# Hybrid SSD and attention layer: the attention values projected for eight heads at a time

## The chip, the cores and the metric

The kernel runs on one core of a Trainium2 chip. The metric is the device time of one execution in microseconds (us), as the median of several runs. TensorE is called PE in the rows, its weight loads PEld, VectorE DVE, ScalarE ACT, GpSimd POOL, and SyncE, which issues most DMAs, SP.

## The reference: what is computed

One decoder layer on 512 tokens of width 1024, all in float32. The part that matters here:

```
h = rms_norm(x, norm_mix_w)
z, xbc, dt, q, k, v, f = split(h @ w_in)       # q, k, v: 16 heads of 64 columns
y_ssd = ssd_mixer(xbc, z, dt, ...)             # chunked scan, 2 groups of 8 heads
y_fox = softmax(qk/8 + cum_i - cum_j, causal) @ v   # "fox" attention, 16 heads
x = x + concat(y_ssd, y_fox) @ w_out
x = x + mlp(rms_norm(x, norm_ffn_w))           # w_up, conv, gate, w_down
```

## The kernel before, in words

Every float32 product is made of three matmuls of rounded operands (`mm3`, line 117): a weight tile is split into a high part `wh` (a CAST on ACT, line 110) and a low part `wl` (a subtraction on DVE or POOL, line 111), the activations `xh`, `xl` likewise, and high by high, high by low and low by high are added in one PSUM bank. `load_split` does the loading: a DMA of 128x1024 from SP's queue, the CAST, the subtraction. There are four buffers for split weights; `LOW_PART` says for each projection which engine subtracts ("d" DVE, "p" POOL).

The attention works on 16 heads in pairs, and on four groups of four heads. For a group, `qk_proj` projects q and k with `wide_block`: two passes over the four weight tiles, each pass with two banks of 128 tokens by 512 columns, all four split tiles being held until the second pass has used them. The values of a group were projected by `v_proj` with `token_block`: two weight tiles one after the other, two banks that each hold two blocks of 128 tokens by 256 columns, so each matmul has 256 columns. Its banks are called `pq`, those of `wide_block` `pw`, those of the output projection `po`.

Of a pair, `fox_qk` turns q and k (`qkT`) and writes `qs`, `ks`; of a head, `fox_bias` and `fox_scores` make the scores (`S`) and their exponentials (`prob`), `fox_turn` turns these (`pT`, copied by ACT to `pt`), and `fox_values` multiplies a pair's `pt` by the values `v` into the bank `o`, which ACT and DVE copy to `mfh` and `mfl`, the operands of the output projection. A bank of `po` is emptied by an addition to `x2` on DVE (line 263). There are three banks for all projections and four for the small tiles.

The order of the work is made by a scheduler, which places instructions on each engine by priority. What stands under `urgent()` (the scan of the SSD heads and all steps of the attention heads) goes first; the projections fill the gaps. The table `fillers` says behind which head a projection is released: "q1" is q and k of group 1, "v1" its values, "o0" and so on the output projection of attention pairs, "a0" and "a1" that of the second SSD group. The values of group 0 were projected before the attention began, beside the end of the second SSD scan (`yd`, `yo`, `st`, `yT` are its matmuls).

Of the kernel before, what the change touches and what calls it, by code (L numbers as in the profile page):

```python
# [8 lines left out]
F32 = mybir.dt.float32  # L9
F32R = mybir.dt.float32r  # L10
AF = mybir.ActivationFunctionType
# [4 lines left out]
P = 128  # L16
SEQ = 512
# [11 lines left out]
HD = 64  # L29
# [14 lines left out]
    "qk1": "dppd",  # L44
    "qk2": "pppd",
    "qk3": "dppd",
    "v0": "dd",
    "v1": "pd",
    "v2": "pd",
    "v3": "pd",  # L50
    "z1": "pdpd",
}
C_MIX, C_SCW, C_SCB, C_FCW, C_FCB, C_QW, C_KW, C_END = 0, 8, 56, 68, 200, 244, 245, 246
# [3 lines left out]
def tile_hybrid_layer(  # L57
# [37 lines left out]
    def low_part(key):  # L95
        order = LOW_PART.get(key, "p")
        n = taken.get(key, 0)
        taken[key] = n + 1
        return dve if order[n % len(order)] == "d" else pool
# [3 lines left out]
    def load_split(src, sub=None, four=True):  # L103
        r = wp.tile([P, 1024], F32, tag="wraw", name="wraw", bufs=3)
        nc.sync.dma_start(r, src)
        where = pa if four and loads[0] % 4 == 3 else wp
        loads[0] += 1
        h = where.tile([P, 1024], F32R, tag="wh", name="wh", bufs=3 if where is wp else 1)
        l = where.tile([P, 1024], F32R, tag="wl", name="wl", bufs=3 if where is wp else 1)
        act.copy(h, r)  # L110
        (sub or dve).tensor_tensor(out=l, in0=r, in1=raw(h), op=ALU.subtract)  # L111
        return h, l

    def mm3(o, ah, al, bh, bl, start, stop, grouped=True, keep=False):
        kw = {} if grouped else {"skip_group_check": True}
        for n, (a, b) in enumerate(((ah, bh), (ah, bl), (al, bh))):
            ins = pe.matmul(o, a, b, start=start and n == 0, stop=stop and n == 2, **kw)  # L117
            if keep:
                tc.keep_in_program_order(ins)

    def bank(name="g"):
        return pg.tile([P, 512], F32, tag="g", name=name)
# [201 lines left out]
        act.activation(eacs, tokS[:, 1, :, 0:16], AF.Exp)  # L324
        nc.sync.dma_start(dsk, ssd_d[0:1, :].to_broadcast([P, SSD_HEADS]))

    def token_block(src, key="tb"):
        tiles = [bank("pq") for _ in range(2)]
        for kh in range(2):
            h, l = load_split(src[kh], sub=low_part(key))  # L330
            for b in range(2):
                for j in range(4):
                    k = 4 * kh + j
                    for c in range(2):
                        tb = 2 * b + c
                        s = slice(tb * P, (tb + 1) * P)
                        mm3(
                            tiles[b][:, c * 256 : (c + 1) * 256], xh[:, k, s], xl[:, k, s],
                            h[:, j * 256 : (j + 1) * 256], l[:, j * 256 : (j + 1) * 256],
                            k == 0 and c == 0, k == NK - 1, grouped=False,  # L340
                        )
        return tiles

    def wide_block(src, key, use, behind=None):
        ws = []
        for b in range(2):
# [177 lines left out]
            dve.tensor_mul(tv, tv, mt[:, :, None].broadcast_to([P, 16, HD]))  # L524
        return tok[:, 0], tok[:, 1]

    def v_proj(gi):
        tiles = token_block(wv[gi], "v%d" % gi)
        v = pa.tile([P, NTB, 4, HD], F32, tag="v", name="v", bufs=2)
        for b in range(2):  # L530
            for c in range(2):
                tb = 2 * b + c
                o = tiles[b][:, c * 256 : (c + 1) * 256].rearrange("p (h d) -> p h d", d=HD)
                act.activation(v[:, tb], o, AF.Copy, scale=r[:, tb : tb + 1])
        return v

    LO, HI = slice(0, HD), slice(HD, P)
# [70 lines left out]
    def fox_turn(prob):  # L608
        where = {}
        for n, kbs in enumerate(((2,), (1, 3), (0,))):  # L610
            w = sum(SEQ - kb * P for kb in kbs)
            t = mbank("pT")
            pt = pf.tile([P, w], F32, tag="pt%d" % n, name="pt", bufs=4)
            w = 0
            for kb in kbs:
                where[kb] = (pt, w)
                for qb in range(kb, NTB):
                    o = QOFF[qb] + kb * P
                    pe.transpose(t[:, w : w + P], prob[:, o : o + P], ident)  # L619
                    w += P  # L620
            act.copy(pt, t[:, :w])
        return where

    def fox_values(pair, turned, v):
        o = po.tile([P, 512], F32, tag="o", name="o")
        for kb in range(NTB):
            for i, rows in ((1, HI), (0, LO)):
                pt, w = turned[i][kb]
                ins = pe.matmul(  # L629
                    o[rows, kb * P :], v[:, kb, (2 * pair + i) % 4, :], pt[:, w : w + SEQ - kb * P],  # L630
                    start=kb == 0, stop=kb == NTB - 1, skip_group_check=True,
                )
                if (kb, i) != (0, 1):
                    tc.keep_in_program_order(ins)
        mh = pf.tile([P, SEQ], F32R, tag="mfh", name="mfh", bufs=2)
        ml = pf.tile([P, SEQ], F32R, tag="mfl", name="mfl", bufs=2)
        act.copy(mh, o)
        dve.tensor_sub(ml, o, raw(mh))
        return mh, ml
# [16 lines left out]
    def project_v(g):  # L656
        vs[g] = v_proj(g)
# [2 lines left out]
    out_proj((0, 1), m0)  # L660
    with urgent():
        m1 = ssd_scan(1, *st1)
    project_v(0)
    pss_ctx.close()
    pf_ctx = ExitStack()
    pf = pf_ctx.enter_context(tc.tile_pool(name="pf", bufs=1, reuse_waits="tile"))
# [17 lines left out]

    def end_pair(p):
        with urgent():
            mf.append(fox_values(p, [turned.pop(n) for n in (2 * p, 2 * p + 1)], vs[p // 2]))

    fillers = {
        0: ["q1"], 3: ["v1"], 4: ["q2", "v2"], 5: ["o0"], 8: ["q3"], 9: ["a0", "o1"], 10: ["v3"], 12: ["o2"],  # L690
        15: ["a1"],
    }

    def fill(name):
        if name[0] == "a":
# [28 lines left out]
    for half in range(2):  # L724
        c = slice(half * 512, (half + 1) * 512)
        ks = slice(half * 4, half * 4 + 4)
        for tb in range(NTB):
            s = slice(tb * P, (tb + 1) * P)
            with urgent():
                xw = pf.tile([P, 512], F32, tag="xw" if tb % 2 else "cum", name="xw", bufs=2)  # L730
                (dve if (half, tb) == (1, 3) else pool).tensor_tensor(out=xw, in0=x2[:, tb, c], in1=nw[:, c], op=ALU.mult)
                t = mbank("hT")
                for j in range(4):
                    pe.transpose(t[:, j * P : (j + 1) * P], xw[:, j * P : (j + 1) * P], ident)
                tv = t.rearrange("p (j f) -> p j f", j=4)
                act.copy(hh[:, ks, s], tv)
                dve.tensor_sub(hl[:, ks, s], tv, raw(hh[:, ks, s]))
# [231 lines left out]
def _lay_out(i, np):  # L969
    w_in = i["w_in"][0]  # L970
    x = i["x"][0]

    def cols(v):
        return v.reshape(-1, 128).T

    def taps(v):
        t, n = v.shape
        return v.reshape(t, n // 128, 128).transpose(2, 1, 0).reshape(128, -1)

    dt, f = w_in[:, 2560:2576], w_in[:, 5648:5664]  # L980
    dtf = np.concatenate([dt, f], axis=1)
    qw, kw = i["fox_q_norm_w"][0], i["fox_k_norm_w"][0]
    pcol = np.concatenate(
        [
            cols(i["norm_mix_w"][0]), taps(i["ssd_conv_w"][0]), cols(i["ssd_conv_b"][0]),
            taps(i["ffn_conv_w"][0]), cols(i["ffn_conv_b"][0]), np.concatenate([qw, qw])[:, None],
            np.concatenate([kw, kw])[:, None],
        ],
        axis=1,
    )  # L990
    db, fb, al = i["ssd_dt_bias"][0], i["fox_f_bias"][0], i["ssd_a_log"][0]
    one = np.ones(16, np.float32)
    rows = [np.concatenate([one, -one]), np.concatenate([db, fb]), np.concatenate([al, np.zeros_like(al)])]
    pdtf = np.tile(np.stack(rows, axis=1), (4, 1))
    ftri = np.kron(np.triu(np.ones((4, 4), np.float32), 1), np.diag(np.repeat(np.float32([0, 1]), 16)))
    return {
        "x": x,
        "xT": x.T.reshape(8, 128, 512),
        "wdtf": dtf.reshape(8, 128, 32).transpose(1, 0, 2).reshape(128, 256),
        "wz": w_in[:, 0:1024].reshape(4, 2, 128, 2, 512).transpose(3, 0, 2, 1, 4).reshape(2, 4, 128, 1024),  # L1000
        "wxbc": _feature(w_in[:, 1024:2560], np),
        "wqk": w_in[:, 2576:4624].reshape(4, 2, 128, 2, 4, 256).transpose(4, 0, 2, 1, 3, 5).reshape(4, 4, 128, 1024),
        "wv": w_in[:, 4624:5648].reshape(2, 4, 128, 4, 256).transpose(3, 0, 2, 1, 4).reshape(4, 2, 128, 1024),
        "wout": _pairs(i["w_out"][0], np),
        "wup": _feature(i["w_up"][0], np),
        "wdown": i["w_down"][0].reshape(2, 11, 128, 2, 512).transpose(0, 3, 2, 1, 4).reshape(4, 128, 5632),
        "pcol": pcol,
        "norm_ffn_w": i["norm_ffn_w"],
        "pdtf": pdtf,
        "ftri": ftri,  # L1010
        "ssd_norm_w": i["ssd_norm_w"],
        "ssd_d": i["ssd_d"],
    }
# [19 lines left out]
```

## Time and profile before

| what | value |
|---|---|
| median of 3 runs | 803.82 us (803.39 to 804.31) |
| the profiled execution's own time | 802.56 us |
| its span, first to last instruction | 800.8 us |
| PE busy | 793.6 us (99%) |
| DVE, ACT, POOL busy | 554.8, 429.4, 262.5 us |
| granted TensorE clock | 0.999 of full speed |

The span is shorter than the execution's time by what lies ahead of the first and behind the last instruction. The recorded duration of a matmul reaches past the start of the next, since matmuls are pipelined; what one costs in a row of many is the distance from start to start, which the chain of waits and the timeline give.

### The profile page before, as it was taken

To read this page: it belongs to the slowest core of one execution; us is meant where nothing else is said; L and a number is where in the kernel's file an instruction comes from. 1 tells how busy PE (TensorE), PEld (TensorE's weight loads), DVE (VectorE), ACT (ScalarE), POOL (GpSimd) and SP (SyncE) were. 2 spreads that over 40 slices of the span, in tenths; PEclk is the share of its full clock that TensorE was granted. 3 is DMA by queue.
4 is the path that set the end of the run, shared out by engine and by line. 5 is a ranking of instruction groups with operands and counts; after the bars stand their busy time and mean duration, and the time that the engine had idled before them with its cause. 6 is when DMAs were issued, how large, how long until landed. Compare 5 with 4: busy or idle time off the path is not lost.

```text
span 800.8 us, 10949 instructions
## 1 busy us (share of the span) xinstructions
PE 793.6 (99%) x3975; PEld 655.3 (82%) x3975; DVE 554.8 (69%) x869; ACT 429.4 (54%) x787; POOL 262.5 (33%) x266
## 2 busy tenths in 40 slices
PE   9999999999999999999999999999999999999997
PEld 6888877878989798778887878888888888888886
DVE  4798998587567477657764577766766766778744
ACT  6557655472588686573751554443443443556531
POOL 0004362743448265225211424233333233133120
PEclk9999999999999999999999999999999999999999
DMA  8524322431334353323231363223223223299992
GB/s 322 186 74 164 104 80 80 146 131 53 112 113 126 98 154 97 106 66 123 77 117 52 129 188 106 84 100 106 86 99 106 88 98 105 85 256 191 211 191 92
DMA packets 31398, 98.13 MB, mean 123 GB/s; under 512 B 4016, under 2 KB 5104, under 8 KB 31344
## 3 DMA queue, kind: packets, MB, share of 16 engines
q1 hardware_dynamic: 27456, 85.38, 32.4%
q0 software_dynamic: 3456, 11.54, 8.0%
q8 instruction: 31, 0.51, 0.3%
q10 hardware_dynamic: 432, 0.52, 0.2%
q14 instruction: 23, 0.19, 0.1%
HBM read 91.56 MB, written 2.20 MB: 117 GB/s over the span
## 4 chain that ended last, share of the span: by engine, by line
PE 95%; DVE 3%; DMA 1%; issue 0%; ACT 0%; SPq 0%; DVEq 0%
PE up L117 30%; PE pw L117 16%; PE po L117 11%; PE pq L117 6%; PE Y L117 6%; PE g L117 5%; PE Z L117 4%; PE X L117 4%; PE o L629 2%; PE pT L619 2%; PE yd L458 2%; PE j L117 1%; PE S L596 1%; PE S L597 1%; DVE xs L397 1%; PE qkT L548 1%
## 5 line engine op out<-in xcount | busy, mean ns | idle before, releaser
L110 ACT CAST wh<-wraw 128x1024 fp32r<-128x1024 f32 x103 | 108.0, 1050 | 123.6 <-PE up L117 74.9
L117 PE MATMUL up<-hh,wh 128*128 128x512 f32 (+1 forms) x360 | 138.6, 385 | 0.3 <-DVE up L826 0.3
L117 PE MATMUL up<-hl,wh 128*128 128x512 f32 (+1 forms) x360 | 138.9, 386 | 0.0
L117 PE MATMUL up<-hh,wl 128*128 128x512 f32 (+1 forms) x360 | 138.5, 385 | 0.0
L111 DVE TENSOR_TENSOR wl<-wraw,wh 128x1024 fp32r<-128x1024 f32 x83 | 107.6, 1297 | 20.8 <-ACT wh L110 20.2
L111 POOL TENSOR_TENSOR wl<-wraw,wh 128x1024 fp32r<-128x1024 f32 x20 | 48.7, 2436 | 95.4 <-ACT wh L110 87.1
L117 PEld LDWEIGHTS up<-hh,wh 128*128 128x128 f32 x360 | 67.6, 188 | 14.2 <-PE up L117 0.7
L117 PEld LDWEIGHTS up<-hl,wh 128*128 128x128 f32 x360 | 67.6, 188 | 13.6 <-issue 0.2
L117 PEld LDWEIGHTS up<-hh,wl 128*128 128x128 f32 x360 | 67.6, 188 | 13.5 <-issue 0.2
L117 PE MATMUL pw<-wh,xh 128*128 128x512 f32 x192 | 77.4, 406 | 0.0
L117 PE MATMUL pw<-wl,xh 128*128 128x512 f32 x192 | 76.0, 396 | 0.0
L117 PE MATMUL pw<-wh,xl 128*128 128x512 f32 x192 | 75.3, 395 | 0.0
L826 DVE TENSOR_TENSOR up<-up,R 128x512 f32<-128x512 f32 x44 | 30.2, 691 | 59.3 <-PE up L117 57.6
L831 DVE SCALAR_TENSOR_TENSOR ua<-up,pc,ua 128x511 f32<-128x511 f32 (+1 forms) x88 | 66.6, 761 | 1.4
L598 DVE CUSTOM_DVE_ANT_0 prob<-S,prob 128x128 f32<-128x128 f32 (+1 forms) x64 | 30.3, 488 | 30.8 <-PE S L597 28.8
L787 ACT CAST wh<-T 128x1024 fp32r<-128x1024 f32 (+1 forms) x30 | 29.3, 977 | 36.8 <-PE Z L117 15.3
L788 DVE TENSOR_TENSOR wl<-T,wh 128x1024 fp32r<-128x1024 f32 (+1 forms) x30 | 33.7, 1133 | 19.1 <-ACT wh L787 18.8
L841 POOL TENSOR_TENSOR ua<-ua 128x512 f32<-128x512 f32 x11 | 15.0, 1363 | 91.0 <-DVE ua L831 91.0
L263 DVE TENSOR_TENSOR x<-po,x 128x512 f32<-128x512 f32 x48 | 32.7, 687 | 17.6 <-PE po L117 17.2
L602 ACT ACTIVATE prob<-prob,nm 128x128 f32<-128x128 f32 (+1 forms) x64 | 35.8, 561 | 16.8 <-DVE nm L598 16.4
L117 PEld LDWEIGHTS pw<-wh,xl 128*128 128x128 f32 x192 | 36.1, 188 | 7.4
L117 PEld LDWEIGHTS pw<-wh,xh 128*128 128x128 f32 x192 | 36.1, 188 | 7.3 <-issue 0.5
(235 smaller groups left out, 1908.7 us busy)
## 6 DMA issues: line engine op xcount, KB each, us to landing
wraw<-in_wup_dram SPq DMA_DIRECT2D x44, 512.0 KB, 3.3
T<-in_wdown_dram POOLq DMA_DIRECT2D x20, 512.0 KB, 7.6
wraw<-in_wqk_dram SPq DMA_DIRECT2D x16, 512.0 KB, 3.4
wraw<-in_wout_dram SPq DMA_DIRECT2D x16, 512.0 KB, 3.4
wraw<-in_wxbc_dram SPq DMA_DIRECT2D x11, 512.0 KB, 5.4
wraw<-in_wdown_dram SPq DMA_DIRECT2D x10, 512.0 KB, 3.7
T<-in_wdown_dram SPq DMA_DIRECT2D x10, 512.0 KB, 5.8
wraw<-in_wz_dram SPq DMA_DIRECT2D x8, 512.0 KB, 3.4
```

What stands on the lines that cost most here:

```text
L110: act.copy(h, r)
L111: (sub or dve).tensor_tensor(out=l, in0=r, in1=raw(h), op=ALU.subtract)
L117: ins = pe.matmul(o, a, b, start=start and n == 0, stop=stop and n == 2, **kw)
L263: dve.tensor_add(dst, banks[tb], dst)
L458: pe.matmul(yd[:, h * HD : (h + 1) * HD], sc[:, h, :], xdt[:, h * HD : (h + 1) * HD], start=True, stop=True)
L598: dve.tensor_tensor_reduce(out=p, in0=sps[:, :n], in1=p, scale=-1.0, scalar=-NEG, op0=ALU.add, op1=ALU.min, accum_out=nm[:, qb : qb + 1],)
L602: act.activation(p, p, AF.Exp, scale=-1.0, bias=nm[:, qb : qb + 1], accum_out=sm[:, qb : qb + 1])
L619: pe.transpose(t[:, w : w + P], prob[:, o : o + P], ident)
L787: act.copy(h[:, :n], src[:, :n])
L788: dve.tensor_tensor(out=l[:, :n], in0=src[:, :n], in1=raw(h[:, :n]), op=ALU.subtract)
L826: dve.tensor_mul(xp, o, R2)
L831: dve.scalar_tensor_tensor(out=a[:, s:], in0=xp[:, : SEQ - s], scalar=pc[:, cw + 2 - s : cw + 3 - s], in1=a[:, s:], op0=ALU.mult, op1=ALU.add,
```

## The change

`token_block` is removed. `v_proj` now makes the values of two groups (eight heads) at a time with `wide_block`: 512 columns in a matmul, two passes, four weight tiles held. The value tile is twice as wide, and there are two of them (`vs[p // 4]`) instead of four. The weights `wv` are laid out anew in memory, with the same bytes. The first values are no longer made before the attention but as its first filler, and the fillers are in another order. To make room, two of the three kinds of `pt` tiles have three buffers instead of four, and the tile `xw` of the following norm uses theirs.

```diff
-    "v0": "dd",
-    "v1": "pd",
-    "v2": "pd",
-    "v3": "pd",
+    "v0": "dpdp",
+    "v1": "dpdp",
...
-    def token_block(src, key="tb"):
...
-    def v_proj(gi):
-        tiles = token_block(wv[gi], "v%d" % gi)
-        v = pa.tile([P, NTB, 4, HD], F32, tag="v", name="v", bufs=2)
-        for b in range(2):
-            for c in range(2):
-                tb = 2 * b + c
-                o = tiles[b][:, c * 256 : (c + 1) * 256].rearrange("p (h d) -> p h d", d=HD)
-                act.activation(v[:, tb], o, AF.Copy, scale=r[:, tb : tb + 1])
+    def v_proj(both):
+        v = pa.tile([P, NTB, 8, HD], F32, tag="v", name="v", bufs=2)
+
+        def take(tb, o):
+            act.activation(v[:, tb], o.rearrange("p (h d) -> p h d", d=HD), AF.Copy, scale=r[:, tb : tb + 1])
+
+        wide_block(wv[both], "v%d" % both, take)
         return v
...
-            pt = pf.tile([P, w], F32, tag="pt%d" % n, name="pt", bufs=4)
+            pt = pf.tile([P, w], F32, tag="pt%d" % n, name="pt", bufs=4 if n == 0 else 3)
...
-    project_v(0)
     pss_ctx.close()
...
-    fillers = {
-        0: ["q1"], 3: ["v1"], 4: ["q2", "v2"], 5: ["o0"], 8: ["q3"], 9: ["a0", "o1"], 10: ["v3"], 12: ["o2"],
-        15: ["a1"],
-    }
+    fillers = {0: ["v0"], 1: ["q1"], 3: ["q2"], 5: ["v1"], 7: ["o0"], 8: ["q3"], 9: ["a0", "o1"], 12: ["o2"], 15: ["a1"]}
...
-                xw = pf.tile([P, 512], F32, tag="xw" if tb % 2 else "cum", name="xw", bufs=2)
+                xw = pf.tile([P, 512], F32, tag="pt1" if tb % 2 else "pt2", name="xw", bufs=3)
```

How the order of instructions moves is shown at three places; numbers behind names tell tiles apart, and line numbers of after are lower by two here and by some twenty further down.

PE at the beginning of the first value projection, of before: `po` is the output projection of the first SSD group, `yT` a step of the second SSD scan.

```order
L117 MATMUL po_1614<-wl_1576,msh_696 128x512
L117 MATMUL po_1614<-wh_1575,msl_697 128x512
L117 MATMUL pq_1859<-wh_1863,xh_93 128x256
L117 MATMUL pq_1859<-wl_1864,xh_93 128x256
L117 MATMUL pq_1859<-wh_1863,xl_94 128x256
```

The same place of after:

```order
L115 MATMUL po_1614<-wl_1576,msh_696 128x512
L115 MATMUL po_1614<-wh_1575,msl_697 128x512
L115 MATMUL pw_1982<-wh_1986,xh_93 128x512
L115 MATMUL pw_1982<-wl_1987,xh_93 128x512
L115 MATMUL pw_1982<-wh_1986,xl_94 128x512
```

The values follow the same output projection in both; although they are a filler of the attention now, the scheduler puts them beside the end of the scan again, in matmuls of 512 columns. There are 384 matmuls `pq` in before and 192 more `pw` in after, and no other matmul is added or removed.

SP's queue from there on, of before; `wraw` are weight loads (by the name of what they read: `wv` values, `wqk` q and k, `wout` output projection), `cum` the bias of a head, `ks` the second half of a pair's k operand.

```order
L105 DMA wraw<-in_wv_dram 128x1024 x2
L105 DMA wraw<-in_wqk_dram 128x1024 x4
L105 DMA wraw<-in_wv_dram 128x1024 x2
L568 DMA cum<-cf_d 128x512 x2
L105 DMA wraw<-in_wqk_dram 128x1024
L568 DMA cum<-cf_d 128x512 x4
L563 DMA ks<-ks 64x1024
L105 DMA wraw<-in_wqk_dram 128x1024 x2
L563 DMA ks<-ks 64x1024
```

Of after:

```order
L103 DMA wraw<-in_wv_dram 128x1024 x4
L103 DMA wraw<-in_wqk_dram 128x1024 x3
L548 DMA cum<-cf_d 128x512 x4
L103 DMA wraw<-in_wqk_dram 128x1024
L548 DMA cum<-cf_d 128x512 x2
L103 DMA wraw<-in_wqk_dram 128x1024 x3
L543 DMA ks<-ks 64x1024 x2
L548 DMA cum<-cf_d 128x512
L103 DMA wraw<-in_wqk_dram 128x1024
L548 DMA cum<-cf_d 128x512
```

Four value tiles are loaded at once, the second group's q and k come behind them, and the third pair's `ks` with them. Counted on PE, 437 matmuls of 512 columns in `po` and `pw` stand between the first scores of head 4 and the last of the last pair's `o` in after; in before 389 of them and 192 of 256 columns stand there. The scores, `pT`, `qkT` and `o` between them are the same in number.

PE behind the last pair's `o`, of before. The output projection of the last pairs there is `po_4475` and the banks that follow; `mfh_4465` is the last pair's operand, `mfh_4300` that of the pair before it.

```order
L117 MATMUL po_4475<-wh_4471,mfl_4466 128x512
L117 MATMUL po_4483<-wh_4471,mfh_4300 128x512
L117 MATMUL po_4483<-wl_4472,mfh_4300 128x512
L117 MATMUL po_4483<-wh_4471,mfl_4301 128x512
L117 MATMUL po_4483<-wh_4471,mfh_4465 128x512
L117 MATMUL po_4483<-wl_4472,mfh_4465 128x512
L117 MATMUL po_4483<-wh_4471,mfl_4466 128x512
L117 MATMUL po_4491<-wh_4471,mfh_4300 128x512
```

Of after, where the last pair's operand is `mfh_4263` and `mfl_4264` and the pair before it has `mfh_4098`:

```order
L115 MATMUL po_4289<-wh_4269,mfl_4099 128x512
L115 MATMUL po_4273<-wh_4269,mfh_4263 128x512
L115 MATMUL po_4273<-wl_4270,mfh_4263 128x512
L115 MATMUL po_4281<-wh_4269,mfh_4263 128x512
L115 MATMUL po_4281<-wl_4270,mfh_4263 128x512
L115 MATMUL po_4289<-wh_4269,mfh_4263 128x512
L115 MATMUL po_4289<-wl_4270,mfh_4263 128x512
L115 MATMUL po_4273<-wh_4269,mfl_4264 128x512
L115 MATMUL po_4281<-wh_4269,mfl_4264 128x512
L115 MATMUL po_4289<-wh_4269,mfl_4264 128x512
L115 MATMUL po_4297<-wh_4269,mfh_4098 128x512
```

In before a bank is finished before the next is begun, and the next but two stands 13 matmuls behind it; 26 matmuls on other operands stand between `o` and the first that reads `mfh_4465`. In after three matmuls stand between `o` and the first that reads `mfh_4263`, the three banks are finished one behind the other, and `po_4297`, which reuses the bank of `po_4273`, stands three places behind the last matmul of that bank.

## Rows read from the trace of the kernel before

**Rows 1.** The page: span, busy time of each engine, and the granted clock by slices.

```profile
span 800.8 us, 10949 instructions
...
PE 793.6 (99%) x3975; PEld 655.3 (82%) x3975; DVE 554.8 (69%) x869; ACT 429.4 (54%) x787; POOL 262.5 (33%) x266
...
PEclk9999999999999999999999999999999999999999
```

**Rows 2.** The waits, PE alone: total us, times, longest.

```profile
PE g L201 <- DVE mhalf L137: 1.0, 1, 1.0
PE g L211 <- ACT xh L188: 0.7, 1, 0.7
PE up L117 <- DVE up L826: 0.3, 1, 0.3
PE yT L491 <- DVE y L488: 0.2, 1, 0.2
```

**Rows 3.** Busy time by stretches: length, PE, PEld, DVE, ACT, POOL, clock, DMA.

```profile
100.00:150.00 50.00, 49.80 (x254) 39.79 (x253) 43.26 (x54) 29.57 (x73) 26.91 (x18) 1.00 0.26 90
...
199.00:216.00 17.00, 17.00 (x137) 16.30 (x136) 9.29 (x14) 7.70 (x15) 5.56 (x3) 1.00 0.34 117
...
262.00:330.00 68.00, 68.00 (x408) 57.44 (x405) 45.03 (x108) 49.84 (x110) 31.83 (x42) 1.00 0.37 110
330.00:404.00 74.00, 74.00 (x434) 61.27 (x433) 46.88 (x102) 44.66 (x93) 21.75 (x29) 1.00 0.32 101
```

**Rows 4.** Groups by form: one of the three `pq`, of 128 each.

```profile
L117 PE MATMUL pq<-wh,xh 128*128 128x256 f32 x128 | 37.0, 289 | 0.0
```

**Rows 5.** The chain of waits: start, us, what, for unbroken runs of matmuls.

```profile
187.80 7.23 PE po L117 x31
...
205.18 7.37 PE pq L117 x62
...
282.12 3.93 PE pw L117 x17
...
353.82 4.81 PE pw L117 x21
...
398.93 2.27 PE pq L117 x19
...
420.62 1.09 PE pT L619 x10
...
467.95 223.28 PE up L117 x984
```

**Rows 6.** Timeline of PE about a group of transposes: start, us.

```profile
127.99 0.60 PE L374 MATMUL xT<-ident,xs 128*128 128x128 f32 x4
128.35 0.48 PE L117 MATMUL pw<-wh,xh 128*128 128x512 f32 x1
128.66 0.40 PE L117 MATMUL pw<-wl,xh 128*128 128x512 f32 x1
```

**Rows 7.** Groups of ACT, DVE and POOL from 199 to 450 us.

```profile
L110 ACT CAST wh<-wraw 128x1024 fp32r<-128x1024 f32 x33 | 34.5, 1048 | 26.3 <-PE po L117 18.5 <-POOL xw L731 4.5 <-PE pw L117 2.9
L512 ACT ACTIVATE tok<-pw,r 128x512 f32<-128x512 f32 x12 | 8.3, 688 | 1.7 <-PE pw L117 1.5
L534 ACT ACTIVATE v<-pq,r 128x256 f32<-128x256 f32 x16 | 6.7, 472 | 6.5 <-PE pq L117 6.5
...
L111 DVE TENSOR_TENSOR wl<-wraw,wh 128x1024 fp32r<-128x1024 f32 x19 | 24.8, 1303 | 7.5 <-ACT wh L110 7.4
...
L111 POOL TENSOR_TENSOR wl<-wraw,wh 128x1024 fp32r<-128x1024 f32 x14 | 33.8, 2415 | 72.8 <-ACT wh L110 64.4 <-DVE x L263 7.4 <-DVE nm L598 1.0
```

**Rows 8.** DMA issues of the value weights: KB each, median us to landing.

```profile
wraw<-in_wv_dram SPq DMA_DIRECT2D x8, 512.0 KB, 4.2
```

**Rows 9.** Timeline where a `po` bank is emptied: PE's last matmul, DVE's addition.

```profile
434.94 0.40 PE L117 MATMUL po<-wh,msl 128*128 128x512 f32 x1
...
435.17 0.40 PE L117 MATMUL po<-wh,mfh 128*128 128x512 f32 x1
...
435.37 0.69 DVE L263 TENSOR_TENSOR x<-po,x 128x512 f32<-128x512 f32 x1 [0.71 <-PE po L117]
```

**Rows 10.** Timelines behind the last `o`: PE's next matmuls, then the copies.

```profile
429.74 0.50 PE L117 MATMUL po<-wl,msh 128*128 128x512 f32 x1
430.08 0.39 PE L117 MATMUL po<-wh,msl 128*128 128x512 f32 x1
430.31 0.39 PE L117 MATMUL po<-wh,msh 128*128 128x512 f32 x1
430.54 0.40 PE L117 MATMUL po<-wl,msh 128*128 128x512 f32 x1
...
429.86 0.59 ACT L637 CAST mfh<-o 128x512 fp32r<-128x512 f32 x1 [6.91 <-PE o L629]
...
430.48 0.69 DVE L638 TENSOR_TENSOR mfl<-o,mfh 128x512 fp32r<-128x512 f32 x1 [2.47 <-ACT mfh L637]
```

**Rows 11.** Timeline of PE, the first scores of head 4.

```profile
265.98 0.22 PE L596 MATMUL S<-ks,qs 128*128 128x128 f32 x1
```

More of the change, by code (lines that the diff above doesn't have):

```diff
@@ L325, in dt_f @@
         nc.sync.dma_start(dsk, ssd_d[0:1, :].to_broadcast([P, SSD_HEADS]))
-    def token_block(src, key="tb"):
-        tiles = [bank("pq") for _ in range(2)]
-        for kh in range(2):
-            h, l = load_split(src[kh], sub=low_part(key))
-            for b in range(2):
-                for j in range(4):
-                    k = 4 * kh + j
-                    for c in range(2):
-                        tb = 2 * b + c
[L336 to L342, printed above, removed]
     def wide_block(src, key, use, behind=None):
@@ L525, in qk_proj @@
         return tok[:, 0], tok[:, 1]
-    def v_proj(gi):
-        tiles = token_block(wv[gi], "v%d" % gi)
-        v = pa.tile([P, NTB, 4, HD], F32, tag="v", name="v", bufs=2)
-        for b in range(2):
-            for c in range(2):
-                tb = 2 * b + c
-                o = tiles[b][:, c * 256 : (c + 1) * 256].rearrange("p (h d) -> p h d", d=HD)
-                act.activation(v[:, tb], o, AF.Copy, scale=r[:, tb : tb + 1])
+    def v_proj(both):
[3 more added lines that the diff above has]
+        wide_block(wv[both], "v%d" % both, take)
         return v
@@ L629, in fox_values @@
                 ins = pe.matmul(
-                    o[rows, kb * P :], v[:, kb, (2 * pair + i) % 4, :], pt[:, w : w + SEQ - kb * P],
+                    o[rows, kb * P :], v[:, kb, (2 * pair + i) % 8, :], pt[:, w : w + SEQ - kb * P],
                     start=kb == 0, stop=kb == NTB - 1, skip_group_check=True,
@@ L686, in end_pair @@
         with urgent():
-            mf.append(fox_values(p, [turned.pop(n) for n in (2 * p, 2 * p + 1)], vs[p // 2]))
-    fillers = {
-        0: ["q1"], 3: ["v1"], 4: ["q2", "v2"], 5: ["o0"], 8: ["q3"], 9: ["a0", "o1"], 10: ["v3"], 12: ["o2"],
-        15: ["a1"],
-    }
+            mf.append(fox_values(p, [turned.pop(n) for n in (2 * p, 2 * p + 1)], vs[p // 4]))
+    fillers = {0: ["v0"], 1: ["q1"], 3: ["q2"], 5: ["v1"], 7: ["o0"], 8: ["q3"], 9: ["a0", "o1"], 12: ["o2"], 15: ["a1"]}
     def fill(name):
@@ L1002, in _lay_out @@
         "wqk": w_in[:, 2576:4624].reshape(4, 2, 128, 2, 4, 256).transpose(4, 0, 2, 1, 3, 5).reshape(4, 4, 128, 1024),
-        "wv": w_in[:, 4624:5648].reshape(2, 4, 128, 4, 256).transpose(3, 0, 2, 1, 4).reshape(4, 2, 128, 1024),
+        "wv": w_in[:, 4624:5648].reshape(4, 2, 128, 2, 512).transpose(3, 0, 2, 1, 4).reshape(2, 4, 128, 1024),
         "wout": _pairs(i["w_out"][0], np),
```

## The prediction

> **What bounds the kernel now.** I read the page first: the span is 800.8 us and PE is busy for 793.6 of it, while DVE, the next, is at 69%; the granted clock is full in every slice (2.4 GHz, the upper of its two levels) [rows 1]. A busy PE can still be a PE that waits inside its instructions, so I read the waits of PE next: in the whole span it waited four times, 2.2 us in all; by their lines two of the waits belong to the start (the warm-up and the first projection), and only 0.2 us (a `yT` of the scan) and 0.3 us (the first `up`) come later [rows 2]. The stretches say the same: from 199 to 404 us, where all value projections lie, PE is never idle, while ACT is busy for 49.84 of 68 us and for 44.66 of 74 us and DVE for 45.03 and 46.88 [rows 3]. So in the part that changes, PE's own instructions are the time. What is taken from PE's stream is gained; what is taken from DVE, ACT, POOL or the DMAs is worth nothing as long as it is not late; and every new wait of PE is lost in full.
>
> **The matmuls.** The recorded 289 ns of a `pq` matmul [rows 4] overlap its neighbours and can't be multiplied. What counts is the chain's unbroken runs, by length over number: `pq` 7.37/62 = 118.9 ns and 2.27/19 = 119.5; `pw` 4.81/21 = 229.0 and 3.93/17 = 231.2; the same shape in `po` 7.23/31 = 233.2, and in `up` 223.28/984 = 226.9 [rows 5]. There were 3 x 128 = 384 `pq` [rows 4], and 192 more `pw` take their place. I take 119 and 230: 384 x 0.119 = 45.70 us go, 192 x 0.230 = 44.16 us come, a gain of 1.54 us. Two narrow matmuls cost 238, a wide one 230: the columns are the same and take the same time, only 8 ns of fixed cost per pair go. Bounds: 118.9 against 233.2 gives 4.6 ns per pair, 0.9 us; 119.5 against 226.9 gives 12.1 ns, 2.3 us. I stay at 1.54, since the blocks of values will stand where the `pw` rows were taken.
>
> The Trainium skill (TensorE: Matmul & The Clock Gate, Back-to-back issue gap) gives the isolated gap of a matmul at the full clock as N/2.4 + 2.5 ns, so a fixed part of 2.5 ns; an estimate by it is 2.5 ns per pair, 0.5 us in all. The trace disagrees: 119 and 230 ns leave a fixed part of 8 ns.
>
> **The breaks between kinds of matmul.** I looked whether each group of small transposes between wide matmuls costs a penalty, for the order has four groups less by my count. Four transposes and the wide matmul behind them take 128.66 - 127.99 = 0.67 us [rows 6]; at 1.09/10 = 0.11 us a transpose in a run of ten [rows 5] and 0.23 for the matmul it is 0.67 without any penalty. So nothing is gained there.
>
> **Weights, their loads and splits.** Eight loads of 512 KB stay eight, 4.2 us to landing [rows 8], but four are issued at once and the q and k of the next group stand behind them on SP, and the `ks` copies of a pair behind those. A first pass uses a weight tile in 12 matmuls, 2.8 us; a tile is split in 1.05 us (ACT) plus 1.30 (DVE) or 2.42 (POOL) [rows 7]. Alternating "dpdp" keeps each engine below one split per 2.8 us. One subtraction moves from DVE to POOL in sum, ahead of a PE that does not ask for it before the tile's turn. I cost this at nothing; its cover is the earlier block on PE, and without it a split that came a whole POOL step late would cost 2.4 us at a block's start.
>
> **The evictions.** 16 activations of 0.472 us become 8 of the size of `tok`, 0.688 [rows 7]: 7.6 us of ACT become 5.5. ACT has a quarter of its time free there [rows 3], so nothing on the path. A `token_block` bank was full 24 matmuls ahead of the other; the two banks of a wide pass are full together, but so they are for q and k, whose evictions are two activations each and made PE wait nowhere [rows 2]. Nothing.
>
> **The buffers.** `pt` with three buffers instead of four: a pair's two tiles are freed when its `o` is done, two heads before the third buffer is wanted again. `xw` gets three buffers for two. Nothing.
>
> **The tail.** The order shows one new squeeze, behind the last `o`. First the copies: in before the next matmul stands at 429.74, the copy to `mfh` ends at 429.86 + 0.59 = 430.45 and the fourth matmul starts at 430.54 [rows 10]. In after three matmuls stand between, so the first that needs `mfh` comes just in time; it needs `mfl` six matmuls later, and this ended at 431.17, before 429.74 + 9 x 0.233 = 431.8. No wait. Then the banks: a bank's last matmul starts at 434.94, the addition that empties it ends at 435.37 + 0.69 = 436.06 [rows 9], 1.12 us later. In after the matmul that takes the bank again stands three places behind, 3 x 0.233 = 0.70 us. PE waits 0.42 us, from where nothing hides it: all behind it on PE is pushed by as much. Bounds: nothing if the additions start earlier than in [rows 9]; 0.69 more if another addition stands ahead on DVE, 1.1 us.
>
> **The second scan.** Around 100 to 150 us DVE is busy for 43.26 of 50 us, and the 0.2 us wait lies there [rows 2, 3]. The scheduler has shifted the steps of the scan against the matmuls by some places either way, a matmul being 0.23 us. A few of these steps had little room; I take nothing, with 0.2 us to gain, and to lose as much as three places at two steps, 1.4 us.
>
> **The sum.** -1.54 + 0.42 = -1.1 us. The profiled execution took 802.56 us, 1.26 below the median of the runs shown; the change should move both alike: 801.4 for such an execution, 802.7 for the median. That is 0.14%; a change of less than 0.2% (1.6 us) I call no change, which is about what a measurement of this kernel can tell.
>
> **The rivals.**
> *The wide matmuls run as well as those of `up`.* If the values run at 226.9 ns, or the narrow ones cost more among the heads than in the runs that I divided, the gain is up to 2.3 us, with 0.2 us from the scan and no wait at the tail 2.5 us: 801.3 us. For it: `up` has the same shape and reaches it over 984 matmuls [rows 5]. Against it: no run of `pw` does. It needs 10.5 ns per pair (2.0 us less 0.42) to pass the 1.6 us, or 8.4 ns without the wait. Chance 0.34.
> *Nothing is gained.* The fixed part is 2.5 ns per pair as by the rule, or 4.6 as by the slowest `po` run, 0.5 to 0.9 us, and the wait at the tail and a place or two in the scan take it back: 803.8 us. For it: the wait at the tail is in the order. Chance 0.14.
> *Slower: the attention heads run out of room.* Two wide blocks, values and q and k of group 1, now stand ahead of the third pair, so head 4 starts later, and its remaining 12 heads have less time. In before its first scores start at 265.98 [rows 11] and the last `o` ends at 429.74 [rows 10], 163.8 us; PE work in between falls from 389 wide and 192 narrow matmuls (112.3 us) to 437 wide (100.5), 11.8 us less. If the chain of the heads through ACT, DVE and POOL can't go faster than it did, PE stands idle for what is missing, at most 11.8 us: 814.5 us. It decides for slower from 2.7 us on. Against it: PE never waited for a head [rows 2], ACT is busy for 73% and 60% of the time there, and 8% more of it still fits [rows 3]. For it: ACT's queue is held up in order, its CASTs waited 18.5 us for `po` matmuls to free the weight buffers [rows 7], and what is behind a CAST are the exponentials and copies that a head needs. Chance 0.09.
>
> **How the numbers follow.** The forecast, 802.7 us, has 0.43; its own range is 802.2 to 803.4. Faster by over 0.2% is the first rival and a little of the forecast's lower edge, 0.36. Slower by over 0.2% is the third, 0.09. The rest is 0.55. The range runs from the first rival, 801.2, to where two of the small waits of scan and tail (1.4 and 0.7) are lost with the smallest gain, 804.6; outside lie most of the third rival and the end of the first.
>
> **What would show it.** The matmuls `pq` are gone and `pw` has 768, in runs of 229 to 231 ns. PE's waits stay few; a new one of about 0.4 us stands at a `po` matmul that waits for `x` (the addition), just behind the last `o`. No wait of PE for a split tile, for `mfh` or for `S`. ACT loses 2 us. The granted clock stays full. I am wrong if PE waits for more than 1 us between 199 and 404 us, or if runs of `pw` in the value blocks are outside 227 to 233 ns.

## The result: slower by a quarter of a per cent

The changed kernel took 804.60 us in the median of 20 runs (802.02 to 806.25) against 802.31 us of 20 runs of the kernel before, the three shown ahead included: a ratio of 1.0024 (1.0014 to 1.0033). In two later comparisons with before the same kernel stood at 1.0009 (0.9995 to 1.0022, so no change is not excluded there) and 1.0025 (1.0013 to 1.0038). The forecast, 802.7 us, was wrong: the sum had a gain of 1.1 us, and the medians show a loss of 0.6 to 2.7 us. That 804.60 lies at the upper end of the prediction's range says nothing for it: the range was reckoned from 803.82 us, the median of three runs of before. Reckoned from the 802.31 us of 20 runs it ends at 803.1.

The page of the profiled execution (803.65 us) answers to [rows 1]:

```profile
span 801.9 us, 10562 instructions
...
PE 792.6 (99%) x3783; PEld 644.6 (80%) x3783; DVE 560.9 (70%) x868; ACT 427.3 (53%) x779; POOL 258.3 (32%) x267
...
PEclk9999999999999999999999999999999999999999
```

The 192 matmuls are gone (3975 to 3783) and PE is busy for 1.0 us less, but the span is 1.1 us longer. So PE waits for longer; its waits answer to [rows 2]:

```profile
PE st L452 <- DVE xdt L450: 1.5, 1, 1.5
PE g L199 <- DVE mhalf L135: 1.0, 1, 1.0
PE g L115 <- ACT wh L181: 0.9, 1, 0.9
PE yT L472 <- DVE y L469: 0.4, 1, 0.4
PE po L115 <- DVE x L261: 0.3, 1, 0.3
...
```

The new and largest wait, 1.5 us at an `st` (the matmul of a scan step's new state, which reads `xdt`, a product that DVE makes for it), is not in the part of the program that the diff touches: it stands at 110 us, in the scan of the first SSD group, some 90 us ahead of the first value projection. The wait at a `po` for `x` is the predicted one at the tail. The wait of `up` for DVE [rows 2] is gone.

The stretches that answer to [rows 3], and one more, 404 to 450 us, in which the last heads lie (columns as there):

```profile
100.00:150.00 50.00, 48.15 (x246) 38.35 (x245) 43.78 (x56) 30.14 (x74) 22.20 (x18) 1.00 0.26 85
199.00:216.00 17.00, 17.00 (x80) 13.77 (x80) 8.88 (x12) 5.42 (x9) 5.50 (x7) 1.00 0.28 94
262.00:330.00 68.00, 68.00 (x354) 54.92 (x353) 41.98 (x88) 45.37 (x91) 32.47 (x33) 1.00 0.37 110
330.00:404.00 74.00, 74.00 (x395) 58.94 (x394) 54.31 (x121) 48.33 (x107) 27.84 (x41) 1.00 0.34 100
404.00:450.00 46.00, 45.59 (x243) 35.35 (x240) 30.72 (x60) 20.20 (x42) 11.60 (x8) 1.00 0.23 69
```

Where the values are, from 199 to 404 us, PE is never idle, as before. It stands still for 1.85 us between 100 and 150 us, where it stood still for 0.20 [rows 3], and for 0.41 us in the last stretch.

### The profile page after: what moved, and what is told of

It reads as the page before. It is cut to its first block, busy times and chain, and to the rows that moved or that the text cites. A ratio compares the mean times of both kernels' runs of the same rounds, so it can differ in the third digit from the quotient of the medians.

```text
span 801.9 us, 10562 instructions
## 1 busy us (share of the span) xinstructions
PE 792.6 (99%) x3783; PEld 644.6 (80%) x3783; DVE 560.9 (70%) x868; ACT 427.3 (53%) x779; POOL 258.3 (32%) x267
## 4 chain that ended last, share of the span: by engine, by line
PE 91%; DVE 4%; DMA 2%; ACT 1%; issue 1%; SPq 0%; POOL 0%; DVEq 0%; POOLq 0%; ACTq 0%
PE up L115 30%; PE pw L115 20%; PE po L115 11%; PE Y L115 6%; PE X L115 4%; PE Z L115 4%; PE g L115 3%; PE o L609 2%; PE pT L599 2%; PE j L115 1%; PE S L576 1%; PE yd L439 1%; PE S L577 1%; DMA sc<-cs_d 1%; PE qkT L528 1%
## 5 line engine op out<-in xcount | busy, mean ns | idle before, releaser
L115 PE MATMUL pw<-wl,xh 128*128 128x512 f32 x256 | 101.5, 396 | 0.0
L115 PE MATMUL pw<-wh,xh 128*128 128x512 f32 x256 | 101.2, 402 | 0.0
L115 PE MATMUL pw<-wh,xl 128*128 128x512 f32 x256 | 101.2, 397 | 0.0
L109 POOL TENSOR_TENSOR wl<-wraw,wh 128x1024 fp32r<-128x1024 f32 x21 | 51.0, 2429 | 75.0 <-ACT wh L108 75.0
L115 PEld LDWEIGHTS pw<-wl,xh 128*128 128x128 f32 x256 | 48.2, 188 | 9.9 <-issue 0.7
L115 PEld LDWEIGHTS pw<-wh,xl 128*128 128x128 f32 x256 | 48.1, 188 | 9.8 <-issue 0.2
L115 PEld LDWEIGHTS pw<-wh,xh 128*128 128x128 f32 x256 | 48.1, 188 | 9.6 <-issue 0.5
```

## A table by stages

The runs of one kernel differ by up to 4 us, and the traces show where: ahead of the first matmul `j` (about 23 us; `j` is the bank of the projections that end the kernel's start). Behind it, profiles of one kernel agree within 0.6 us. So I divided every profile at three starts: the first `j`, the first matmul of the values, the last `po`. All in us; the last column is the sum of the three stages behind `j`.

| kernel | start to `j` | `j` to values | values to last `po` | last `po` to end | behind `j` |
|---|---|---|---|---|---|
| before | 23.07 | 176.38 | 248.40 | 352.94 | 777.72 |
| before, longer warm-up | 21.23 | 176.57 | 248.39 | 352.99 | 777.95 |
| after | 23.12 | 180.37 | 245.39 | 353.00 | 778.76 |
| after, 2nd profile | 21.83 | 180.27 | 245.91 | 353.03 | 779.21 |
| after, 3rd profile | 24.11 | 180.28 | 245.38 | 352.96 | 778.62 |
| after, longer warm-up | 22.43 | 180.30 | 245.38 | 352.92 | 778.60 |
| after, z1 exchanged | 24.84 | 179.77 | 245.37 | 352.95 | 778.09 |
| after, heads' reach 1500 | 21.98 | 176.28 | 249.19 | 352.85 | 778.32 |
| before, reach 2250 | 24.60 | 180.68 | 246.08 | 353.00 | 779.76 |
| narrow values, new places | 23.22 | 176.26 | 253.27 | 352.92 | 782.45 |
| reach 1500, q3 first | 22.92 | 176.26 | 247.79 | 353.04 | 777.09 |
| the same, longer warm-up | 22.19 | 176.28 | 247.79 | 353.04 | 777.11 |
| heads still earlier, longer warm-up | 22.26 | 176.27 | 247.90 | 353.12 | 777.29 |
| after, z1's third subtraction on DVE | 23.05 | 178.94 | 254.65 | 352.92 | 786.50 |

One thing must be known to read it: in the kernels with 179.7 to 180.7 us in the second stage, the first value matmul stands behind 16 `yd` and four `yT` that elsewhere stand behind it. Twenty small matmuls at 0.11 us [rows 5] are 2.2 us, which are to be moved from the second stage to the third. With this, after loses 180.3 - 2.2 - 176.4 = 1.7 us ahead of the values and gains 248.4 - (245.4 + 2.2) = 0.8 us behind them, 0.5 us less in one of its four profiles (the second, where a score waits for a `ks` copy); in sum it is 0.9 to 1.5 us longer behind `j`.

## The experiments

**Theory A** says that the loss comes from the order of the start and the first scan. The scheduler puts what stands under `urgent()` ahead by `AHEAD` = 2000 places. The changed program is shorter, and ahead of the steps that start the later heads (numbers 8 and up) 96 to 192 matmuls fewer stand; so the same 2000 places reach further towards the program's start, and from some length on the order of PE's first rows, of SP's loads and of the whole first scan becomes another one. In the programs' order that is seen row by row: the kernel before has one early order for 1000, 1500 and 2000 places, and for 2250 and 2500 PE's rows up to the first value matmul are those of after; after with 1500 has the early order of before, also when only the steps of heads 8 and up get the 1500, and it keeps its own when only heads 0 to 3 get them. **Theory B** says that the wide blocks or the new places of the fillers cost the time where they stand.

**1. Only the heads' reach shortened, in the changed kernel.**

```diff
     def start_head(n):
         qs, ks = pairs[n // 2]
-        with urgent():
+        with tc.high_priority(1500):
```

> The changed kernel, but the steps that start a head are put ahead by 1500 places instead of 2000. Its order of instructions then equals that of the kernel before on all engines up to the first value projection. Theory A (the loss is the new order of the start and the first scan, which cost 2.0 us in the profiles between 100 and 112 us; the wide values gain 1.7 us where they stand): the wait of st for xdt (1.5 us) is gone and the kernel takes 2 us less than the changed one, so 0.5 us less than before to equal, a ratio of 0.999 to 1.000. Theory B (the wide blocks or their new places cost the time, between 199 and 450 us): it stays 1.5 to 2.3 us above before, a ratio of 1.002 to 1.003.

803.45 us, a ratio of 1.0008 (0.9992 to 1.0024). The wait of `st` is gone and the second stage is that of before, 176.28 us: here theory A holds. But the total did not fall by 2 us; three waits now stand in the last heads' stretch that before does not have:

```profile
PE S L576 <- DVE x L261: 0.9, 1, 0.9
PE po L115 <- ACT mfh L617: 0.7, 1, 0.7
PE po L115 <- DVE x L261: 0.3, 1, 0.3
```

**2. Only the reach lengthened, in the kernel before.**

```diff
-AHEAD = 2000
+AHEAD = 2250
```

> The kernel before with all urgent steps put ahead by 2250 places instead of 2000, nothing else; values in 256 columns at their old places. Its order then equals that of the changed kernel up to the first value projection. Theory A: st waits for xdt by about 1.5 us near 110 us and the kernel is slower than before by 2.0 to 2.8 us, a ratio of 1.0025 to 1.0035. Theory B: no wait that counts, a ratio of 0.9995 to 1.0005.

805.61 us, 1.0032 (1.0017 to 1.0047), with the values as narrow and as placed as in before. The wait:

```profile
PE st L471 <- DVE xdt L469: 1.8, 1, 1.8
```

Behind `j` it is 2.04 us longer than before, and nearly all of it ahead of the values: 180.68 - 2.2 - 176.38 = 2.1 us. The early order of after alone makes the kernel before slower by 2 us behind `j`: for the scan theory A is shown, without any change of the values.

**3. Narrow values at the new places, with the new buffers.** The values are made by `token_block` again, two groups one behind the other into a tile of eight heads; fillers and buffers are those of after. This program is long enough to keep the early order of before.

```diff
-        wide_block(wv[both], "v%d" % both, take)
+        for g in range(2):
+            tiles = token_block(wv[2 * both + g], "v%d" % both)
```

> The changed kernel with its places, buffers and value tiles of eight heads, but the values in matmuls of 256 columns again (384 instead of 192). The longer program keeps the order of before up to the first values. Theory A: no wait of st, no gain in columns, at the tail up to 0.5 us: 0 to 0.7 us slower than before, a ratio of 1.000 to 1.001. Theory B, if the places cost: 1.9 us and the 1.7 us of the columns on top, 1.0025 to 1.0045; if only the width of the blocks costs: 1.000.

808.36 us, 1.0074 (1.0053 to 1.0095), more than either theory allowed. The third stage is 4.9 us longer than before. Over half of that is one place where the scheduler has put `o` and `qkT` in turns (nine changes between the two kinds in this program, one in before, three in after); PE's timeline there:

```profile
294.21 1.07 PE L628 MATMUL o<-pt,v 128*64 128x512 f32 x2
295.21 0.33 PE L547 MATMUL qkT<-ident,tok 128*128 128x128 f32 x1
...
299.63 0.44 PE L547 MATMUL qkT<-ident,tok 128*128 128x128 f32 x2
```

From 294.21 to 299.63 us are 5.4 us for a pair's 16 `o` and four `qkT`; the last pair's 16 `o` in after take 2.3 us (435.06 to 437.37, below) and four transposes 0.44. So this cost 2.7 us. The rest, 2.2 us, goes with the same three waits at the last heads as in the first run. What follows is that the new places are not free, and that this run can't price the columns, since its order among the heads is another one than the first run's.

**4. The changed kernel again.**

> The changed kernel once more beside the others, so that all are compared on one chip: a ratio of 1.0024 by both theories.

803.61 us, 1.0009 (0.9995 to 1.0022), less than the 1.0024 expected; behind `j` 779.21 us. In this profile a score of the last heads waits for the copy of `ks` by DMA, which no other profile of after shows:

```profile
407.64 0.30 PE L576 MATMUL S<-ks,qs 128*128 128x128 f32 x1 [0.33 <-DMA ks<-ks]
```

By the medians, 803.45 and 803.61 us, the first run is not faster than after beyond the noise: what it gains in the scan it loses at the last heads.

**5. Reach 1500 and q3 ahead of o0.** Why should the last heads cost something? In after head 4 starts at 284.72 us (265.98 before, [rows 11]):

```profile
284.72 0.22 PE L576 MATMUL S<-ks,qs 128*128 128x128 f32 x1
```

The heads then catch up, but the last `o` starts at 437.16 us instead of 429.54, when 42 matmuls of the output projection are left instead of 71. So I released q and k of the last four heads earlier, and gave the reach of 1500 to all urgent steps, where the first run gave it to the starts of heads alone:

```diff
-AHEAD = 2000
+AHEAD = 1500
-    ... 7: ["o0"], 8: ["q3"], ...
+    ... 7: ["q3"], 8: ["o0"], ...
```

> The changed kernel with all urgent steps put ahead by 1500 places (the start and first scan then have the order of before, as in the first run) and, new, with the fillers q3 and o0 exchanged: q and k of the last group are released at head 7, the output projection o0 at head 8. By its order the last pair's o then has 71 matmuls of the output projection behind it, as in before, where the changed kernel has 42. Theory A, now with two parts (scan order 2.0 us, tail 1.0 to 2.4 us because the last heads come when the fillers are used up, columns a gain of 1.7 us): no wait of PE for st, S, mfh or x, and counted from 30 us on 1.7 us less than before, 0.9978 to 0.999 as a ratio. Theory B (wide blocks or their places cost something between 199 and 404 us whatever the tail): 0 to 1 us above before, 1.000 to 1.001.

802.04 us, 0.9999 (0.9986 to 1.0012), not the 0.9978 to 0.999 expected. Behind `j` it is 0.63 us shorter than before and 1.23 shorter than the first run, so the last heads have a part besides the scan; but of the columns' gain (1.6 us by the chain, below) only 0.63 is left. One wait of a `po` stays, at 398 us:

```profile
PE po L115 <- ACT mfh L617: 0.4, 1, 0.4
```

**6. The same with a longer warm-up.**

```diff
-WARM = 8
+WARM = 11
```

> The run just above with 11 instead of 8 warm-up matmuls at the start, which work on constants; the order is otherwise the same. In the traces so far the first matmuls that need data run at 0.43 us from start to start instead of 0.23 for 0 to 8 us, after PE stood still for 0.6 to 1.1 us between 5.5 and 7.5 us, and this alone moves everything behind it by -1.2 to +1.6 us from run to run. If the pause brings it, the longer warm-up shortens the pause and the runs lie closer together and about 1 us lower than those of the kernel just above; if not, the first data matmul only starts later and the time is the same or up to 0.5 us longer, with the same spread of 3 to 4 us.

800.69 us, 0.9986 (0.9974 to 0.9997), the one version that is below both kernels; 11 runs lie within 2.7 us (the 12 of the fifth within 4.2). Behind `j` it is the fifth run to 0.02 us. The gain came as expected, but not by a shorter pause: ahead of its data matmuls PE waits longer here than in the profile of the fifth run (1.1 us for an `xh`, where that has 0.5 for a `wh`).

**7. The changed kernel a third time.**

> The changed kernel a third time, beside the two above: 1.0009 to 1.0024 by the two comparisons so far; the runs above should be 3 us lower by theory A, 1 us by theory B.

804.42 us, 1.0025 (1.0013 to 1.0038), 2.4 us above the fifth run beside it, between the 1 us of theory B and the 3 of theory A.

**8. What holds `xdt` up: DVE's queue or POOL?** In after DVE takes 3.74 us for two pieces of `xs` ahead of the `xdt` that `st` waits for:

```profile
104.17 3.74 DVE L378 SCALAR_TENSOR_TENSOR xs<-xp,half_w,xs 128x511 f32<-128x511 f32 x2
107.83 0.68 DVE L475 TENSOR_TENSOR msl<-yT,msh 128x512 fp32r<-128x512 f32 x1
108.44 0.73 DVE L378 SCALAR_TENSOR_TENSOR xs<-xp,half_w,xs 128x509 f32<-128x509 f32 x1
109.09 0.68 DVE L442 TENSOR_TENSOR y<-yd,y 128x512 f32<-128x512 f32 x1
109.69 0.98 DVE L450 TENSOR_TENSOR xdt<-xdt,dte 128x512 f32<-128x512 f32 x1
```

Beside them POOL, and then PE:

```profile
104.97 2.40 POOL L109 TENSOR_TENSOR wl<-wraw,wh 128x1024 fp32r<-128x1024 f32 x1 [2.41 <-ACT wh L108]
```

```profile
110.82 1.10 PE L452 MATMUL st<-xdt,b_tok 128*128 128x512 f32 x2 [1.45 <-DVE xdt L450]
```

The third piece, alone, takes 0.73 us. The second started at 104.94, 0.03 us ahead of POOL's subtraction, and ended at 107.91, 0.54 us behind it.

```diff
-    "z1": "pdpd",
+    "z1": "dppd",
```

> The changed kernel with two subtractions of the second group's z weights exchanged between DVE and POOL, so that PE's and SP's orders are the same instruction by instruction, but DVE has one subtraction (1.2 us) less ahead of the xdt that st waits for near 110 us, and POOL runs two of them there. If the wait is the length of DVE's queue alone, st waits 0.3 us instead of 1.5. If it is that DVE's pieces of xs take 1.4 to 1.9 us instead of 0.75 while POOL subtracts, the wait stays at 1 us or more, since POOL subtracts for longer.

`st` waits 1.1 us. On DVE and then on POOL:

```profile
101.44 2.96 DVE L378 SCALAR_TENSOR_TENSOR xs<-xp,half_w,xs 128x509 f32<-128x509 f32 x1
...
107.93 2.35 DVE L378 SCALAR_TENSOR_TENSOR xs<-xp,half_w,xs 128x509 f32<-128x509 f32 x1
```

```profile
101.46 2.39 POOL L109 TENSOR_TENSOR wl<-wraw,wh 128x1024 fp32r<-128x1024 f32 x1
...
107.34 2.40 POOL L109 TENSOR_TENSOR wl<-wraw,wh 128x1024 fp32r<-128x1024 f32 x1 [2.05 <-ACT wh L108]
```

Each of POOL's two subtractions holds one piece of `xs` up until it is done, and DVE's saved subtraction does not make up for it.

**9 and 10. Both kernels with the longer warm-up.**

> The kernel before with 11 instead of 8 warm-up matmuls, otherwise the same order. It tells how much of the gain of the run with the longer warm-up comes from the warm-up alone. If the pause of PE at the start brings the low rate of the first matmuls: about 1 us below before, 0.998 to 0.9993, and from the first j to the end 777.7 us as before, within 0.3. If the longer warm-up does nothing here, 0.9995 to 1.0005, and the gain of that run is all of columns, scan and tail.

> The changed kernel with 11 warm-up matmuls. Three profiles of the changed kernel show 778.6 to 779.2 us from the first j to the end, before 777.7. Theory A: the same 1.1 us above before from the first j on, with the waits of st (1.4 us) and x (0.3 us); if besides this the new order of the first rows costs something at the start, the run is more than 1.1 us above the kernel before with the same warm-up. As a ratio to before 1.000 to 1.0015.

801.28 us, 0.9993 (0.9981 to 1.0005), and 802.92 us, 1.0010 (1.0000 to 1.0021). Behind `j` 777.95 and 778.60 us, as without it. The gain of 0.9 us for before was expected, but its interval reaches beyond no change. Side by side with the same warm-up after is 1.6 us longer in the median, 0.65 of it behind `j` in these two profiles. Beside 801.28 us the sixth run's 800.69 is 0.6 us less, in another group of runs: some of its gain over before may be the warm-up's.

**11. Heads still earlier.** q3 at head 7, o0 at 9, o1 at 11, a0 at 12, o2 at 14.

> The kernel with reach 1500, the longer warm-up and a filler table that puts q3 to head 7, o0 to 9, o1 to 11, a0 to 12 and o2 to 14, so that heads 12 to 15 start 2 to 5 us earlier by the order. With o0 alone behind q3 there were 777.1 us from the first j to the end, with 0.6 us lost at 398 us to a wait for mfh. If the tail costs because the last heads come late: that wait is gone and 776.0 to 776.6 us are left, 1.2 to 1.7 below before; if the fillers' own operands are what is late, 777 us or more with a wait for mfh elsewhere. As a ratio to before 0.997 to 0.9985.

801.20 us, 0.9997 (0.9987 to 1.0006), and 777.29 us behind `j`, not the 776.0 to 776.6 expected. The wait for `mfh` is gone, but a pair's `o` waits for DVE instead, and the third stage is 247.90 us as against 247.79:

```profile
PE o L609 <- DVE mfl L618: 0.8, 1, 0.8
```

Earlier heads alone don't win more.

**12. POOL's subtraction taken away from beside the `xs` piece.**

```diff
-    "z1": "pdpd",
+    "z1": "pddp",
```

> The changed kernel with the third subtraction of the second group's z weights moved from POOL to DVE, where it stands behind the xdt that st waits for near 110 us; PE's order is the same up to and beyond that st, and so is DVE's up to and beyond that xdt. If st waits because POOL's subtraction (2.40 us from 104.97) holds up one piece of xs on DVE (2.97 us instead of 0.73): that piece takes about 0.75 us, xdt is ready 2.2 us earlier and st does not wait (0 to 0.2 us). If the wait is the length of DVE's queue, which is unchanged there, st waits 1.4 us as before. The order behind it is another one, with 18 changes between o and qkT in the attention heads, so the total may be several us longer and tells nothing here.

DVE, and then PE:

```profile
104.00 1.52 DVE L378 SCALAR_TENSOR_TENSOR xs<-xp,half_w,xs 128x511 f32<-128x511 f32 x2
105.44 0.69 DVE L475 TENSOR_TENSOR msl<-yT,msh 128x512 fp32r<-128x512 f32 x1
106.04 0.74 DVE L378 SCALAR_TENSOR_TENSOR xs<-xp,half_w,xs 128x509 f32<-128x509 f32 x1
106.69 0.69 DVE L442 TENSOR_TENSOR y<-yd,y 128x512 f32<-128x512 f32 x1
107.29 0.68 DVE L450 TENSOR_TENSOR xdt<-xdt,dte 128x512 f32<-128x512 f32 x1
```

```profile
109.04 1.02 PE L452 MATMUL st<-xdt,b_tok 128*128 128x512 f32 x2
```

The same five rows of DVE in the same order, and the two pieces take 1.52 us instead of 3.74; `xdt` is done at 107.97 instead of 110.67 and `st` does not wait. The wait is POOL's subtraction, not the length of DVE's queue. The lost time does not come back in this run, though: its first value matmul stands where before has it, and its second stage is still 2.6 us longer (178.94 and 176.38), with a new wait of 1.2 us at a `pw` and 0.8 at a `yT`. The whole took 811.32 us, a single execution; that the 18 changes between `o` and `qkT` made most of it is not shown.

## Why the prediction was wrong, step by step

**The step that failed is the scan.** It said: "A few of these steps had little room; I take nothing, with 0.2 us to gain, and to lose as much as three places at two steps, 1.4 us." The loss was 1.7 us, more than the bound, and no rival had it. The stretch I looked at was right; that I called it the second scan was not, since at 100 to 150 us it is the first group's. I had seen that the scheduler shifts these steps, and priced the shift in places of a matmul, 0.23 us each. But the shift moves other engines against each other too: it set POOL's subtraction (2.40 us) beside a piece of `xs` on DVE, which cost 2.2 us on DVE. In before `st` started at 107.88 with its `xdt` done at 106.59:

```profile
105.91 0.68 DVE L469 TENSOR_TENSOR xdt<-xdt,dte 128x512 f32<-128x512 f32 x1
```

```profile
107.88 1.02 PE L471 MATMUL st<-xdt,b_tok 128*128 128x512 f32 x2
```

That slack of 1.3 us was less than what came. Runs 2 and 12 show both links, from the reach to the order, and from POOL to the wait.

**The matmuls** were right. The chain of after has runs of `pw` in the value blocks and behind them, start, us and number:

```profile
206.60 9.37 PE pw L115 x41
...
217.28 6.89 PE pw L115 x30
...
258.77 19.12 PE pw L115 x83
```

That is 228.5, 229.7 and 230.4 ns, within the 227 to 233 that the prediction named. Taken together they give 229.7 ns, and the two narrow runs 119.0 [rows 5]; by these the 192 pairs gain 1.6 us, against 1.54. No run shows this gain by itself, but the runs of matmuls leave the columns no part in the loss.

**Evictions, weights and buffers** cost nothing there, as forecast: PE waits for nothing between 199 and 404 us. Behind that one profile of four has the wait of a score for `ks` (run 4), which the prediction had ruled out. The eight evictions, in answer to [rows 7]:

```profile
L512 ACT ACTIVATE v<-pw,r 128x512 f32<-128x512 f32 x8 | 5.2, 682 | 4.4 <-PE pw L115 4.3
```

**The tail** was right in place and size, but it was not all. Behind the last `o`, PE's timeline (compare [rows 10]):

```profile
435.06 2.38 PE L609 MATMUL o<-pt,v 128*64 128x512 f32 x16
437.37 0.51 PE L115 MATMUL po<-wh,mfh 128*128 128x512 f32 x1
...
439.61 0.85 PE L115 MATMUL po<-wh,mfl 128*128 128x512 f32 x3
440.79 0.50 PE L115 MATMUL po<-wh,mfh 128*128 128x512 f32 x1 [0.32 <-DVE x L261]
```

DVE there, in answer to [rows 9, 10]:

```profile
438.10 0.69 DVE L618 TENSOR_TENSOR mfl<-o,mfh 128x512 fp32r<-128x512 f32 x1 [2.00 <-ACT mfh L617]
440.04 1.89 DVE L261 TENSOR_TENSOR x<-po,x 128x512 f32<-128x512 f32 x3 [1.25 <-PE po L115]
```

The copies come in time, and the three banks that are full together make PE wait: from 439.61 the three matmuls are 0.69 us, so the next would have started at 440.30; it starts at 440.79, 0.49 us later (0.42 was forecast). Behind the values after gains 0.8 us where the columns give 1.6: 0.8 us are lost there, this wait among them.

**The third rival, heads without room,** came true in its condition and not in its price. Head 4 started 18.7 us later, the last `o` 7.6 us later; the heads caught up for the most part, and what is lost behind the values besides the bank is 0.3 us, not 2.7 or 11.8; that it is the heads' is not shown. In the first run, with another order among the heads, three waits cost 1.9 us. The fifth run has 1.4 us less in that stage (249.19 to 247.79); whether the reach or the earlier q and k gave it was not separated.

**The sum** after the fact: -1.6 (columns) + 1.7 (scan) + 0.8 (0.49 at the bank, the rest not traced) = +0.9 us, where the profiles behind `j` have +0.9 to +1.5.

**What stays open.** The medians differ by 0.6, 2.3 and 2.7 us in the three comparisons, in two of them by more than this. The rest would lie ahead of the first `j`: with the early order of after it comes at 21.8 to 24.8 us in six profiles, with that of before, and the same warm-up, at 22.0 to 23.2 in four. That the new order of PE's first rows costs something there is likely by these means (23.6 and 22.8), but the spread is as large as the difference, and I did not settle it. Of the 1.0 us that the fifth run does not keep of 1.6, its wait for `mfh` at 398 us is about 0.6; the rest stays open.

## What to carry to other kernels

Where a scheduler makes the order from priorities with a reach, a change in one stage can re-order a stage that the diff does not touch: compare the orders from the first row on, and price each re-ordered step on every engine, not in places of the bound engine. A step whose slack is less than one instruction of another engine (here 1.3 and 2.40 us) can lose it in a new order. And where runs differ by more than the effect, compare the profiles from behind the noisy stage on.

## What the hardware showed that I had not expected

**DVE and POOL hold each other up.** A piece of `xs` takes 0.73 us alone; started beside POOL's subtraction of 128x1024 it took 2.97 us (104.94 to 107.91), that is 2.40 of POOL and 0.57. The pair of pieces took 3.74 us in after, 3.73 in the second run, 3.74 in the tenth, and 1.52 where POOL was free. The Trainium skill (SBUF — State Buffer, Who interferes with whom) says that a DVE instruction with two inputs in SBUF contends with a GpSimd instruction that reads SBUF, and that the one that comes second is blocked for the whole of the other. The trace agrees in the length; but by these rows DVE started first, by 0.02 and 0.03 us, and it was DVE that waited. In before it went the other way: DVE started 0.02 us ahead of POOL's subtraction and ran through in 0.68 us, and POOL took 2.90 us instead of 2.40. Which of two near starts waits can't be told from the start times shown.

```profile
106.51 0.68 DVE L402 SCALAR_TENSOR_TENSOR xs<-xp,xs 128x512 f32<-128x512 f32 x1
...
106.53 2.90 POOL L111 TENSOR_TENSOR wl<-wraw,wh 128x1024 fp32r<-128x1024 f32 x1 [3.85 <-ACT wh L110]
```

**The first matmuls at half rate.** In after the first matmuls on data run at 0.43 us from start to start, after PE had stood still for 0.95 us ahead of 6.91:

```profile
8.34 0.63 PE L210 MATMUL g<-xl,wdt 128*32 128x512 f32 x1
8.77 0.63 PE L115 MATMUL g<-xh,wh 128*128 128x512 f32 x1
...
11.86 0.39 PE L209 MATMUL g<-xh,wdt 128*64 128x512 f32 x1
```

The granted clock there is 0.57 over 8 to 12 us, so at the lower of its two levels (1.2 GHz) for most of it, and 1.00 behind:

```profile
8.00:12.00 4.00, 4.00 (x12) 2.65 (x11) 3.44 (x5) 3.55 (x7) 0.00 (x0) 0.57 1.01 372
12.00:16.00 4.00, 4.00 (x19) 2.77 (x18) 2.95 (x7) 2.70 (x3) 0.00 (x0) 1.00 1.03 420
```

In before, the second run, the fifth and the twelfth the view gives 1.00 beside the same spacing, but the trace has no record of the clock there: its first one, at full clock, begins at 10.5 to 13.4 us, where the spacing of 0.43 us ends, and the view counts a stretch without a record as full. The number of matmuls at this spacing differs by profile, from none to twelve, and so does PE's wait for the first `wh` (none to 2.3 us); with these two the first `j` starts between 21.2 and 24.8 us. In the four profiles with the longer warm-up none is at 0.43 us, and the record starts between 3.9 and 6.7 us, at full clock. A pause alone does not bring the lower clock: in the sixth run PE stood still for 1.1 us ahead of 7.31 and the clock stayed at 1.00.
